# A two-layer decoder trunk: both mixings in finer steps and new orders, and the MLP up product with both parts of x side by side

## The chip, the core and the metric

The kernel runs on one core of one Trainium2 chip. Its time is the device time of one execution in microseconds; 694.61 is the median of three runs. One more execution was taken with the hardware profiler.

## What is computed

One sequence of 256 tokens, width 1024, in float32, goes through two layers and a final norm. Each layer is a mixing and an MLP, each added to x.

```python
for l in range(2):
    z = rms_norm(x, ln_mix[l]) @ w_in[l]
    u_self, q_mem = z[..., :768], z[..., 768:]
    if l == 0:
        self_out = s5_mixer(u_self, ...)      # 48 groups of 16 channels, 64 complex states, then a gated GELU
    else:
        k, v = rope(rms_norm(x, kv_norm) @ w_kv)   # 12 heads of 64
        self_out = causal attention of rope(u_self) over k, v
    mem_out = attention of q_mem (4 heads) over 256 memory tokens, their k, v = rms_norm(mem) @ w_mem_kv[l]
    x = x + concat(self_out, mem_out) @ w_out[l]
    up = causal depthwise conv, width 3, of (rms_norm(x) @ w_up[l])   # 2 x 2816 channels: g, v
    x = x + (silu(g) * v) @ w_down[l]
return rms_norm(x, final_norm)
```

## The kernel before

x is held on chip with its channels on the partitions (8 blocks of 128 by 256 tokens). The weights come by DMA in one fixed order through three raw buffers (class `Stream`). Most products keep float32 accuracy by splitting: ScalarE rounds a weight block to `whi` (line 115), VectorE makes the rest `wlo` (line 119, or 121 where a gain is multiplied in), the activations are split the same way, and `mm3` (lines 249 to 251) multiplies whi with hi, whi with lo and wlo with hi. Weights named in `NATIVE` are not split: they are multiplied as float32, for which the trace shows two instructions to a product. Five pairs of whi and wlo are held at a time.

The first mixing (`layer0`) has these steps, each a letter of the string `ORDER`: P the input product in float32 (line 869), E the powers of the poles, X the input operators (two halves, r and i, for three thirds b = 0, 1, 2 of the channels), T and t their transposes (line 771), V the output operators (array `Vd`), l a local operator that TensorE builds (lines 838 and 841) and L its placing by ScalarE into `Tm`, u and U the input moved to its place, S the states (products at lines 896 and 897, then rotation, scan and rotation back on VectorE, giving `Hs`), Y the outputs (lines 941 and 944, then transposes), G the GELU, K and K1 the memory's keys and values of layer 0 and layer 1 (lines 377 and 381), m the split of the memory for K1, A the four memory heads. Constants such as `E_POOL`, `X_POOL`, `H_DVE`, `U_ACT` say which engine does which piece. TensorE, VectorE and GpSimd issue the steps of `ORDER` exactly in that order. The gate product, the product with w_out and the additions to x follow, ordered by the framework's planner, which puts what is ready first by its place in the program.

`ffn` runs 22 passes: pass f makes two blocks of up channels in one PSUM bank `psU` (48 matmuls of 256 columns), `post` evacuates it, multiplying with the norm `rb` (line 521), convolves (526, 528), gates (532 to 534) and splits (541); from pass 5 on the down product of pass f - 5 follows (24 matmuls of 256 columns in layer 0, 12 of 512 columns at line 557 in layer 1). The banks alternate between two pairs, so four passes can be in flight. The norm enters only at line 521, so TensorE starts before it is known.

The second mixing (`layer1`) has its steps in `ORDER1`: I the input product, X the split for keys and values, K and v these, Q and R the rotary embeddings, h0 to h3 the memory heads, h4 to h15 the causal heads (scores, softmax, transposes at line 458, product with v at lines 470 and 471), O the output product, z the additions to x. Here the planner decides, and the string gives priorities. A head's product with v fills one half of the partitions of its pair's bank.

## Time and profile before

| | |
|---|---|
| median of 3 runs | 694.61 us (694.43 to 701.04) |
| profiled execution | 695.04 us, span 693.3 |
| TensorE matmul busy | 654.1 us, 94% of the span |
| VectorE busy | 565.4 us, 82% |
| ScalarE busy | 413.2 us, 60% |
| GpSimd busy | 132.9 us, 19% |
| mean granted TensorE clock | 0.957 |

PE is TensorE's matmuls, PEld its weight loads, DVE VectorE, ACT ScalarE, POOL GpSimd. Matmuls overlap each other, so how dense TensorE is shows in the distance between their starts, not in the busy time. The granted clock is a share of 2.4 GHz; 0.5 is 1.2 GHz.

### The profile page before, as it was taken

Reading aid. Unit: us, or ns where it says so; the run is one execution under the profiler, and the core shown is the slowest. Engines: PE = TensorE matmul, PEld = TensorE weight load, DVE = VectorE, ACT = ScalarE, POOL = GpSimd, SP = SyncE. Lnnn points to the kernel's source line nnn. Section 1 sums busy time; section 2 is a strip of 40 time slices with the busy share of each in tenths; the row PEclk is TensorE's granted clock in tenths of the full one; section 3 lists DMA queues with packets and bytes.
Section 4 is the critical chain, followed back from the end, with each engine's and each line's share of the span. In section 5 each row is a group of like instructions: output and inputs, shape, how many; then the busy total and the mean of one; then the engine's idle time right before and its main releaser. Section 6 shows DMA issues by size and latency. Waiting matters only on the chain.

```text
span 693.3 us, 12668 instructions
## 1 busy us (share of the span) xinstructions
PE 654.1 (94%) x4904; PEld 616.5 (89%) x4904; DVE 565.4 (82%) x1012; ACT 413.2 (60%) x747; POOL 132.9 (19%) x134
## 2 busy tenths in 40 slices
PE   6369899999999999999999998989999999999995
PEld 5358888998899999999999997868999999999984
DVE  7996999796879998888888798974749999888872
ACT  6368625576556665555557579864636666555631
POOL 5795623402300000000001255500300000000000
PEclk9775879999999999999999999899999999999998
DMA  8610133274455555555555544323625555565401
GB/s 315 245 62 1 61 99 99 93 217 148 152 181 184 183 183 181 186 185 182 182 186 156 168 128 140 107 89 122 213 92 182 181 186 183 183 188 187 172 1 61
DMA packets 43259, 105.13 MB, mean 152 GB/s; under 512 B 3776, under 2 KB 14144, under 8 KB 43200
## 3 DMA queue, kind: packets, MB, share of 16 engines
q1 hardware_dynamic: 42624, 103.74, 45.9%
q8 instruction: 38, 0.62, 0.4%
q10 hardware_dynamic: 576, 0.59, 0.2%
q14 instruction: 21, 0.17, 0.1%
HBM read 103.28 MB, written 1.05 MB: 150 GB/s over the span
## 4 chain that ended last, share of the span: by engine, by line
PE 82%; DVE 12%; DMA 2%; issue 2%; ACT 1%; POOL 0%; SPq 0%; DVEq 0%; ACTq 0%
PE psU L250 12%; PE psU L251 12%; PE psU L249 12%; PE acc L557 9%; PE acc L249 7%; PE acc L250 7%; PE acc L251 7%; PE ps L377 2%; DVE wlo L119 2%; PE ps L381 2%; PE ps L838 1%; DMA s5c<-s5b 1%; PE psO L470 1%; DVE X L638 1%; PE psT L458 1%
## 5 line engine op out<-in xcount | busy, mean ns | idle before, releaser
L115 ACT ACTIVATE whi<-wraw 128x1024 fp32r<-128x1024 f32 (+1 forms) x176 | 182.9, 1042 | 142.4 <-PE psU L250 84.9
L119 DVE TENSOR_TENSOR wlo<-wraw,whi 128x1024 fp32r<-128x1024 f32 (+1 forms) x176 | 217.9, 1240 | 26.7 <-PE acc L251 13.1
L250 PE MATMUL psU<-xlo,whi 128*128 128x256 f32 x704 | 198.6, 282 | 1.4 <-DVE xlo L331 1.4
L251 PE MATMUL psU<-xhi,wlo 128*128 128x256 f32 x704 | 197.8, 282 | 0.0
L249 PE MATMUL psU<-xhi,whi 128*128 128x256 f32 x704 | 197.6, 282 | 0.0
L250 PEld LDWEIGHTS psU<-xlo,whi 128*128 128x128 f32 x704 | 132.9, 189 | 2.5 <-DVE xlo L331 1.8
L249 PEld LDWEIGHTS psU<-xhi,whi 128*128 128x128 f32 x704 | 132.7, 189 | 0.7
L251 PEld LDWEIGHTS psU<-xhi,wlo 128*128 128x128 f32 x704 | 132.6, 189 | 0.0
L528 DVE SCALAR_TENSOR_TENSOR y<-u,held,y 128x254 f32<-128x254 f32 (+1 forms) x176 | 77.8, 477 | 1.5 <-ACT y L526 1.5
L521 DVE TENSOR_TENSOR u<-psU,rb 128x512 f32<-128x512 f32 x44 | 30.3, 688 | 32.4 <-PE psU L251 31.3
L526 ACT ACTIVATE y<-u,held 128x256 f32<-128x256 f32 x88 | 47.6, 589 | 13.0 <-DVE u L521 12.9
L269 POOL TENSOR_TENSOR sq<-sq 128x512 f32<-128x512 f32 x5 | 8.0, 1598 | 226.9 <-DVE held L364 179.1
L251 PE MATMUL acc<-ah,wlo 128*128 128x256 f32 x176 | 49.7, 283 | 0.0
L250 PE MATMUL acc<-al,whi 128*128 128x256 f32 x176 | 49.7, 283 | 0.0
L249 PE MATMUL acc<-ah,whi 128*128 128x256 f32 x176 | 49.6, 282 | 0.0
L869 PE MATMUL acc<-xg,wraw 128*128 128x256 f32 x128 | 34.1, 429 | 5.5 <-ACT xg L859 5.5
L869 PEld LDWEIGHTS acc<-xg,wraw 128*128 128x128 f32 x128 | 27.7, 221 | 10.0 <-ACT xg L859 5.5
L288 POOL TENSOR_TENSOR y<-mf,held 128x1 f32<-128x1 f32 x2 | 1.1, 550 | 180.5 <-DVE mf L1215 180.5
L249 PEld LDWEIGHTS acc<-ah,whi 128*128 128x128 f32 x176 | 33.6, 191 | 0.0
L251 PEld LDWEIGHTS acc<-ah,wlo 128*128 128x128 f32 x176 | 33.5, 191 | 0.0
L250 PEld LDWEIGHTS acc<-al,whi 128*128 128x128 f32 x176 | 33.5, 191 | 0.0
L250 PE MATMUL acc<-xlo,whi 128*128 128x256 f32 x112 | 31.7, 284 | 0.0
(271 smaller groups left out, 1475.1 us busy)
## 6 DMA issues: line engine op xcount, KB each, us to landing
wraw<-w_up SPq DMA_DIRECT2D x88, 512.0 KB, 3.4
wraw<-w_down SPq DMA_DIRECT2D x44, 512.0 KB, 3.4
wraw<-w_out SPq DMA_DIRECT2D x16, 512.0 KB, 3.6
wraw<-w_in SPq DMA_DIRECT2D x15, 512.0 KB, 3.5
wraw<-w_mem_kv SPq DMA_DIRECT2D x8, 512.0 KB, 4.2
wraw<-w_kv SPq DMA_DIRECT2D x6, 512.0 KB, 3.7
wraw<-w_kv SPq DMA_DIRECT2D x8, 384.0 KB, 3.4
wraw<-w_glu SPq DMA_DIRECT2D x6, 384.0 KB, 3.5
```

The lines of the kernel that those rows point to most:

```text
L115: self.nc.scalar.activation(hi[:, c], t[:, c], AF.Copy, scale=1.0 if g_ is None else g_)
L119: self.nc.vector.tensor_sub(lo[:, c], t[:, c], hi[:, c].bitcast(F32))
L249: PE.matmul(out, whi, ahi, start=first, stop=False, skip_group_check=True)
L250: PE.matmul(out, whi, alo, start=False, stop=False, skip_group_check=True)
L251: PE.matmul(out, wlo, ahi, start=False, stop=last, skip_group_check=True)
L377: PE.matmul(pk[:, 256 * m:256 * m + 256], w[i][:, o + 128 * m:o + 128 * m + 128], g[j], start=k + m + i + j == 0, stop=k == KT - 1, skip_g ...
L381: PE.matmul(pv[:, 256 * t:256 * t + 256], g[j][:, 128 * t:128 * t + 128], w[i][:, o + 256:o + 512], start=k + t + i + j == 0, stop=k == KT ...
L521: V.tensor_mul(u, v2(p), rb2(rb))
L526: S.activation(y[:, j], u[:, j], AF.Identity, bias=cp(3), scale=cp(2))
L528: V.scalar_tensor_tensor(y[:, j, d:], u[:, j, :T - d], cp(2 - d), y[:, j, d:], op0=ALU.mult, op1=ALU.add)
L557: PE.matmul(dacc[2 * t + h], a_, w_[:, 512 * i:512 * i + 512], start=False, stop=last and a_ is al, skip_group_check=True)
L869: PE.matmul(acc[2 * h + b][:, 256 * (m % 2):256 * (m % 2) + 256], w[:, 512 * i + 128 * m:512 * i + 128 * m + 128], xg[k // 2][:, k % 2], s ...
```

## The change

- First mixing: a new `ORDER`, with smaller steps (P in halves, l in quarters, each head in four steps with a separate step p for its pair's product with v, the gate product, the output product and the additions in the string too). Behind the bar in the string the planner decides. The weights are streamed in the order of the steps that use them.
- First mixing, engines: all but one of the V operations move from GpSimd to VectorE; three of the four rounds of E1 stay on GpSimd, the fourth goes to VectorE and the fourth round of E0 to GpSimd; one X half is on GpSimd as before, another one; eight of twelve placing copies of U on VectorE go to ScalarE; two evacuations of the transposes and three of Y come to VectorE; all H additions are on VectorE.
- K1 is multiplied in float32: its weights and the memory are no longer split.
- The narrow products of S, Y and l are reordered, so that neighbours go to different column groups of the array; S is cut into halves of 64 columns. The operand `dd` of l is prepared on the host.
- Attention: both heads of a pair are multiplied with v in one step, alternating.
- MLP: in passes 1 to 4 `normalise` makes two blocks each of x times gain times norm, split into hi and lo that lie side by side. From pass 5 on one matmul of 512 columns multiplies whi with both, and one of 256 wlo with hi. Each block of up channels then has a bank of its own, and ScalarE copies one half and VectorE adds the other (no multiplication with the norm).
- Second mixing: a new `ORDER1`, softmax in two steps, one rotary stack moved from GpSimd to VectorE.

```diff
@@ -29,11 +29,13 @@
-NATIVE = (("mkv", 0), ("win", 0))
+NATIVE = (("mkv", 0), ("mkv", 1), ("win", 0))
...
+
+NORMED = 5
...
-P rm0 E0 P rx1 E1 P rx2 E0 P rx3 Xi0 Xr0 E0 V1 u0 t0 V0 V0 Xi1 u1 P B0 T0 D0 V0 Xr1 V1 U1 U0 P U0 l0 U0 T1 E1 U0 E1
-E1 Xi2 Xr2 E0 U1 S0 V1 P t2 S0 T2 S0 L0 U1 L0 P B1 L0 V2 t1 S0 D1 u2 U1 V2 U2 U2 U2 m S1 U2 S2 K S1 K K D2 K rm1 V2
-S1 B2 q l1 S1 L1 L1 rm2 L0 S2 Y0 S2 m S2 K K K K rm3 Y0 K L1 L1 G0 m K1 Y1 G0 Y2 Y1 K1 K1 m Y2 K1 G1 G2 K1 K1 G1 K1
-A G2 A A A A K1 A K1 A
+P E0 P P E1 P P P rm0 E0 Xr0 rx1 P P P rx2 E0 rx3 E0 E1 P Xi0 u0 D0 P U0 T0 U0 P U0 t0 P E1 D2 Xr1 P U0 V0 B0 Xi1 S0
+u1 V0 V0 l0 T1 Xi2 U1 S0 P U1 S0 l0 V2 V1 P V1 L0 V2 t1 K Xr2 B1 S0 L0 T2 U1 K u2 V1 rm1 U2 K U2 U1 L0 L0 Y0 B2 K U2
+t2 U2 E1 S1 V2 l1 D1 l1 l1 l1 L1 rm2 L1 S1 rm3 S2 Y0 S1 S1 K L1 K S2 K S2 Y0 L1 S2 K K1 Y1 K G0 G0 | q Y2 Y2 h1 Y1 h2
+Y1 h1 h3 h3 K1 K1 h0 Y2 h2 G1 h1 G2 h0 K1 K1 h0 K1 G1 h2 G2 h3 h1 h2 h0 K1 h3 K1 g g g g g p1 g0 g0 g g1 p0 g1 p1 K1
+g2 p0 o o o o g2 o o o o z3 z2 z1 z0
 """
-X_POOL = ((0, 1),)
-E_POOL = (1,)
-M_POOL = (1, 2, 3)
-H_DVE = (1,)
-V_DVE = ()
-Y_ACT = (0, 1, 2)
-EVAC_ACT = (0, 1, 2)
-T_ACT = ((0, 0), (0, 1), (1, 0), (1, 1), (2, 0), (2, 1))
-U_ACT = ((1, 1, 1, 0), (0, 1, 1, 1), (1, 0, 1, 1))
+V_POOL = ((2, 2),)
+X_POOL = ((2, 0),)
+E_POOL = ((0, 3), (1, 0), (1, 1), (1, 2))
+H_DVE = (0, 1, 2)
+Y_ACT = (1,)
+EVAC_ACT = (0, 2)
+T_ACT = ((0, 0), (0, 1), (1, 1), (2, 0), (2, 1))
+U_ACT = ((1, 1, 1, 0), (1, 1, 1, 1), (1, 1, 1, 1))
...
+x x x x I I I X r1 r2 I I I I r3 I X Q0 qm Q1 K K Q1 h0 K X h3 X h2 Q2 K h1 h0 K h2 h2 R0 h1 h2 v Q0 R1 v R0 h3 R1 v
+h0 h3 h1 K Q2 h10 h7 h0 h1 h5 v R2 h4 h3 h5 h4 h4 h7 v v h8 h5 h4 h11 h6 h10 h9 v v p0 h6 e0 h9 h10 h6 R2 h13 h5 p1 h7
+h8 h14 h8 h7 h8 h12 h6 p1 p0 e1 h10 h9 h12 O h11 p3 h13 h12 h12 h9 h15 h11 p3 h13 h14 h11 h15 h14 p4 p5 h13 h15 p2 p2
+p5 p4 p6 O h14 O h15 p7 p6 p7 O z0 O O O O z3 z2 z1
...
+    def mem_kv(l, bk, mem, ks, new, vm):
...
+                PE.matmul(pk[:, 256 * m:256 * m + 256], w[:, o + 128 * m:o + 128 * m + 128], mk, start=k + m == 0,
+                          stop=k == KT - 1, skip_group_check=True)
             for t in range(2):
-                for i, j in pairs:
-                    PE.matmul(pv[:, 256 * t:256 * t + 256], g[j][:, 128 * t:128 * t + 128],
-                              w[i][:, o + 256:o + 512], start=k + t + i + j == 0, stop=k == KT - 1,
-                              skip_group_check=True)
...
+    def pv(out, pair, causal):
+
+        for t in range(2):
+            c = 128 if t and causal else 0
+            for h in range(2):
+                v, PT = pair[h]
+                PE.matmul(out[64 * h:64 * h + 64, c:256], v[t], PT[:, t, c:], start=t == 0, stop=t == 1,
+                          skip_group_check=True)
...
+    def head_pair(i, bo, causal, outp, hi, lo):
+
+        po = bo("psO")
+        pv(po, [outp.pop(2 * i + h) for h in range(2)], causal)
+        yield
+        o = po[:, :256]
+        S.activation(hi[i], o, AF.Copy)
+        V.tensor_sub(lo[i], o, hi[i].bitcast(F32))
+        yield
...
+            def normalise(b):
+
+                t = sg([128, 2, T], name="xn")
+                for i in range(2):
+                    k = 2 * b + i
+                    V.scalar_tensor_tensor(t[:, i], x[:, k], gains[:, gi, k:k + 1], rb, op0=ALU.mult, op1=ALU.mult)
+                for i in range(2):
+                    n = sn([128, 2, T], F32R, "xhl")
+                    S.activation(n[:, 0], t[:, i], AF.Copy)
+                    V.tensor_sub(n[:, 1], t[:, i], n[:, 0].bitcast(F32))
+                    hl.append(n)
+
             def post(f, p):
                 u = sl([128, 2, T], name="u")
-                V.tensor_mul(u, v2(p), rb2(rb))
+                if f < NORMED:
+                    V.tensor_mul(u, v2(p), rb2(rb))
+                else:
+                    for j in range(2):
+                        S.activation(u[:, j], p[j][:, T:], AF.Copy)
+                        V.tensor_add(u[:, j], p[j][:, :T], u[:, j])
                 y = sl([128, 2, T], name="y")
                 for j in range(2):
                     c = j * FT + f
@@ -558,15 +583,20 @@
                                   stop=last and a_ is al, skip_group_check=True)
             for f in range(FT):
-                p = (br if f % 2 else bw)("psU")
-                w = [None, None]
-                todo = [(j, k) for j in range(2) for k in range(KT)]
-                for j, k in todo:
-                    if w[j] is None:
-                        w[j] = W.get(("up", l, j * FT + f))
-                    c = slice(128 * k, 128 * k + 128)
-                    mm3(p[:, 256 * j:256 * j + 256], w[j][0][:, c], w[j][1][:, c], *act(k),
-                        k == 0 and j == 0, k == KT - 1)
+                p = (br if f % 2 else bw)("psU") if f < NORMED else [b_("psU") for b_ in (br, bw)]
+                for j in range(2):
+                    whi, wlo = W.get(("up", l, j * FT + f))
+                    for k in range(KT):
+                        c = slice(128 * k, 128 * k + 128)
+                        if f < NORMED:
+                            mm3(p[:, 256 * j:256 * j + 256], whi[:, c], wlo[:, c], *act(k), k == 0 and j == 0, k == KT - 1)
+                        else:
+                            PE.matmul(p[j], whi[:, c], hl[k].rearrange("p a t -> p (a t)"), start=k == 0, stop=False,
+                                      skip_group_check=True)
+                            PE.matmul(p[j][:, :T], wlo[:, c], hl[k][:, 0], start=False, stop=k == KT - 1,
+                                      skip_group_check=True)
+                if 0 < f <= 4:
+                    normalise(f - 1)
                 post(f, p)
                 if LAG <= f < FT - 4 + LAG:
                     dacc = dacc or [ba("acc") for _ in range(4)]
...
         def local_operator(i):
             n, nf = LEN[i], LEN[i] // 4
             Tm[i] = s5.tile([128, n, 4, 32], F32, name=f"Tm{i}")
             G.memset(Tm[i], 0.0)
-            dds = []
-            for q in range(n // 8):
-                d = sv([128, 8, 32], name="dd")[:32]
-                V.tensor_mul(d, ident[:32, None, :32].to_broadcast([32, 8, 32]),
-                             dsk[:, PC[i][0] + 8 * q:PC[i][0] + 8 * q + 8, None].to_broadcast([32, 8, 32]))
-                dds.append(d)
-            p = ba()
+            p = pl[i] = ba()
             for f in range(nf):
+                o = [p[32 * s:32 * s + 32, 128 * f:128 * f + 128] for s in range(4)]
+                for g in range(2):
+                    for s in range(4):
+                        PE.matmul(o[s].rearrange("p (i c) -> p i c", c=32)[:, :, 16 * g:16 * g + 16],
+                                  Bz[i][:, 4 * f + s, g], Vd[i][:, 4 * f + s, g, 0:4], start=g == 0, stop=False,
+                                  tile_position=(0, 32 * s), skip_group_check=True)
                 for s in range(4):
-                    pr = 4 * f + s
-                    o = p[32 * s:32 * s + 32, 128 * f:128 * f + 128]
-                    for g in range(2):
-                        PE.matmul(o.rearrange("p (i c) -> p i c", c=32)[:, :, 16 * g:16 * g + 16],
-                                  Bz[i][:, pr, g], Vd[i][:, pr, g, 0:4], start=g == 0, stop=False,
-                                  tile_position=(0, 32 * s), skip_group_check=True)
-                    PE.matmul(o[:, :32], ident[:32, :32], dds[pr // 8][:, pr % 8], start=False, stop=True,
-                              tile_position=(0, 32 * s), skip_group_check=True)
-            pl[i] = p
+                    PE.matmul(o[s][:, :32], ident[:, 32 * s:32 * s + 32], dsk[:, PC[i][0] // 4 + f], start=False,
+                              stop=True, tile_position=(0, 32 * s), skip_group_check=True)
+                yield
...
@@ -893,8 +915,10 @@
             i, o = piece(b)
             pr, pi = br(), br()
             for j in range(8):
-                PE.matmul(pr[:, 64 * j:64 * j + 64], RT[b][0][:, j], U[b][:, j], start=True, stop=True)
-                PE.matmul(pi[:, 64 * j:64 * j + 64], RT[b][1][:, j], U[b][:, j], start=True, stop=True)
+                for ri, p in enumerate((pr, pi)):
+                    for c in HALF:
+                        PE.matmul(p[c, 64 * j:64 * j + 64], RT[b][ri][:, j, c], U[b][:, j], start=True, stop=True,
+                                  tile_position=(0, c.start), skip_group_check=True)
             yield
             ec, es = E[i][:, 0, o:o + 8], E[i][:, 1, o:o + 8]
             rt = lambda: sr([128, 8, 64], name="rot")
...
@@ -934,21 +958,23 @@
         def outputs(b):
             pc, off = piece(b)
             py = ba("psY")
-            for f in range(2):
-                for s in range(4):
-                    j = 4 * f + s
-                    o = py[64 * f:64 * f + 64].rearrange("p (i s c) -> p s i c", s=4, c=32)[:, s]
-                    PE.matmul(o, U[b][:, j], Tm[pc][:, off + j], start=s == 0, stop=False, tile_position=(0, 64 * f),
-                              skip_group_check=True)
-                    for g in range(2):
-                        PE.matmul(o[:, :, 16 * g:16 * g + 16], Hs[b][:, j, g], Vd[pc][:, off + j, g, 1:5],
-                                  start=False, stop=True, tile_position=(0, 64 * f), skip_group_check=True)
+            for s in range(4):
+                o = [py[64 * f:64 * f + 64].rearrange("p (i s c) -> p s i c", s=4, c=32)[:, s] for f in range(2)]
+                for f in range(2):
+                    PE.matmul(o[f], U[b][:, 4 * f + s], Tm[pc][:, off + 4 * f + s], start=s == 0, stop=False,
+                              tile_position=(0, 64 * f), skip_group_check=True)
+                for g in range(2):
+                    for f in range(2):
+                        PE.matmul(o[f][:, :, 16 * g:16 * g + 16], Hs[b][:, 4 * f + s, g],
+                                  Vd[pc][:, off + 4 * f + s, g, 1:5], start=False, stop=True,
+                                  tile_position=(0, 64 * f), skip_group_check=True)
             yield
             yc = sx([128, 4, 128], name="yc")
...
```

## Rows read from the trace of the kernel before

**Rows 1.** TensorE by time, first mixing: start us, us, line, operation, out<-in, [idle before <-releaser].

```profile
15.97 7.15 PE L869 MATMUL acc<-xg,wraw 128*128 128x256 f32 x32
...
36.69 1.97 PE L771 MATMUL ps<-held,X 128*128 128x128 f32 x8 [11.75 <-DVE X L638]
...
51.65 0.31 PE L841 MATMUL ps<-dd,held 32*32 32x32 f32 x2 [4.07 <-DVE dd L829]
...
183.07 0.28 PE L249 MATMUL psU<-xhi,whi 128*128 128x256 f32 x1
```

**Rows 2.** Stretches: us, then PE, PEld, DVE, ACT, POOL busy (count), clock, DMA, GB/s.

```profile
40.00:60.00 20.00, 15.94 (x97) 12.93 (x97) 19.20 (x42) 16.73 (x45) 12.24 (x26) 0.76 0.17 53
...
300.00:340.00 40.00, 40.00 (x338) 40.00 (x337) 32.70 (x53) 21.85 (x32) 0.00 (x0) 1.00 0.57 185
...
420.00:440.00 20.00, 16.82 (x89) 15.24 (x89) 18.54 (x26) 19.07 (x38) 12.69 (x12) 0.83 0.41 132
```

**Rows 3.** VectorE and GpSimd in order of time, first mixing.

```profile
29.10 4.66 POOL L635 TENSOR_TENSOR Vd<-s5c 128x1024 f32<-128x1024 f32 x2
...
32.01 4.62 DVE L638 TENSOR_TENSOR X<-xt 64x512 f32<-64x512 f32 x2
...
54.14 1.41 DVE L638 TENSOR_TENSOR X<-xt 64x512 f32<-64x512 f32 x2
```

**Rows 4.** VectorE's groups by shape, first MLP: count | busy us, mean ns | idle before.

```profile
L119 DVE TENSOR_TENSOR wlo<-wraw,whi 128x1024 fp32r<-128x1024 f32 x66 | 80.5, 1220 | 10.6 <-PE psU L251 5.5 <-PE acc L251 4.2 <-issue 0.6
...
L521 DVE TENSOR_TENSOR u<-psU,rb 128x512 f32<-128x512 f32 x22 | 15.1, 688 | 14.3 <-PE psU L251 13.3 <-ACT rb L308 1.0
```

**Rows 5.** VectorE's groups by shape, first mixing.

```profile
L121 DVE SCALAR_TENSOR_TENSOR wlo<-wraw,held,whi 128x512 fp32r<-128x512 f32 x8 | 9.6, 1246 | 0.0
```

**Rows 6.** TensorE in order of time, the S5 layer's narrow products.

```profile
78.01 0.33 PE L896 MATMUL ps<-U,RT 128*128 128x64 f32 x2
...
81.75 0.39 PE L897 MATMUL ps<-U,RT 128*128 128x64 f32 x2
...
99.97 0.41 PE L838 MATMUL ps<-Vd,Bz 128*32 128x64 f32 x4
...
108.29 0.43 PE L941 MATMUL psY<-Tm,U 128*64 128x128 f32 x2
...
109.92 0.22 PE L944 MATMUL psY<-Vd,H 128*64 128x64 f32 x1
109.92 0.32 PE L941 MATMUL psY<-Tm,U 128*64 128x128 f32 x1
...
111.87 1.13 PE L377 MATMUL ps<-memT,wraw 128*128 128x256 f32 x4
```

**Rows 7.** TensorE in order of time, one pass of the second MLP.

```profile
567.42 0.62 PE L557 MATMUL acc<-whi,ah 128*128 128x512 f32 x2
...
570.20 0.28 PE L249 MATMUL psU<-xhi,whi 128*128 128x256 f32 x1
...
575.90 0.62 PE L557 MATMUL acc<-whi,ah 128*128 128x512 f32 x2
```

**Rows 8.** The page's DMA issues: count, KB each, us to landing.

```profile
wraw<-w_mem_kv SPq DMA_DIRECT2D x8, 512.0 KB, 4.2
```

**Rows 9.** TensorE in order of time, attention, second mixing.

```profile
461.31 0.65 PE L470 MATMUL psO<-PT,vv 128*64 128x256 f32 x2
...
462.10 0.55 PE L458 MATMUL psT<-held,P 128*128 128x128 f32 x3
...
473.75 0.66 PE L470 MATMUL psO<-PT,vv 128*64 128x256 f32 x4
...
474.56 0.55 PE L458 MATMUL psT<-held,P 128*128 128x128 f32 x3
```

**Rows 10.** VectorE in order of time, the start of either MLP.

```profile
213.60 1.37 DVE L528 SCALAR_TENSOR_TENSOR y<-u,held,y 128x255 f32<-128x255 f32 x3 [0.69 <-ACT y L526]
...
515.56 0.69 DVE L521 TENSOR_TENSOR u<-psU,rb 128x512 f32<-128x512 f32 x1 [5.51 <-PE psU L251]
```

More of the change, by code (lines that the diff above doesn't have):

```diff
@@ L198, in _body, with by_steps @@
     W0 = [((0,), 0), ((1,), 0)] + [(ks, h) for h in range(2) for ks in PAIRS][1:]
[L199 to L205 removed]
+    def by_steps(steps, **lists):
+        its = {n: iter(l) for n, l in lists.items()}
+        return [w for s_ in steps.split() if s_ in its for w in next(its[s_], ())]
+    one = lambda l: [[w] for w in l]
+    w0 = [(("win", 0, ks, h), blocks(a["w_in"][0], ks, 512 * h, 512), (len(ks), 512)) for ks, h in W0]
+    mkv = lambda l: [[(("mkv", l, k // 2), mkv_ap(l, k // 2), (2, 512))] if k % 2 == 0 else [] for k in range(KT)]
+    glu = [(("glu", ks, b), blocks(a["w_glu"], ks, 256 * b, 256), (3, 256)) for ks, b in GLU]
+    order = by_steps(ORDER, P=[w0[:2], []] + [p for w in w0[2:] for p in ([w], [])], K=mkv(0), K1=mkv(1), g=one(glu),
+                     o=one(wout(0)))
+    order += ffn_order(0)
+    order += by_steps(
+        ORDER1, I=one(win(1)),
+        K=one([(("wk", ks, b), blocks(a["w_kv"], ks, 256 * b, 256), (4, 256)) for ks, b in WK]),
+        v=one([(("wv", ks, c), blocks(a["w_kv"], ks, SELF + 384 * c, 384), (2, 384)) for c in range(2) for ks in PAIRS]),
+        O=one(wout(1)))
+    order += ffn_order(1)
     W = Stream(nc, order, rawp, hlp, lambda key: [gains[:, 2 + key[1], 2 * key[2] + i:2 * key[2] + i + 1]
@@ L1050, in layer0, with steps @@
                 calls[f"{n}{b}"] = lambda f=f, b=b: f(b)
+        gens["g"], gens["o"] = gate(), output0()
+        for b in range(3):
+            gens[f"g{b}"] = gated(b)
+        for b in range(4):
+            calls[f"z{b}"] = lambda b=b: residual0(b)
         for i in range(2):
-            calls[f"l{i}"] = lambda i=i: local_operator(i)
+            gens[f"l{i}"] = local_operator(i)
             gens[f"L{i}"] = put_local_operator(i)
-        with tc.manual_schedule(engines=MANUAL):
-            for s in ORDER.split():
+        def steps(text):
+            for s in text.split():
                 if s in gens:
@@ L1091, in layer1 @@
         causal_ops.extend([identb, maskb])
-        act, d = split_x(1), {}
+        sq_, d = [], {}
+        act = split_x(1, steps=sq_)
         rb = pool.tile([128, T], F32, name="rbq")
```

176 lines of the change are left out of this document (73 added, 103 removed).

## Prediction

> **What bounds the kernel now.** I read the stretches of the span first, then each engine in order of time within a stage, then the groups by shape. The reader is to see four stages with different limits. The first mixing lasts until the first `psU` matmul at 183.1 us [rows 1]. TensorE stands still 11.75 us before its first transpose at 36.7 and 4.07 us before line 841 at 51.65 [rows 1]; from there to 183.1 its matmuls follow each other almost without a gap, but dear ones: the granted clock averages 0.76 of full speed between 40 and 60 us [rows 2]. VectorE is busy 19.2 of 20 us there, so both engines are near their limit. The MLPs are TensorE's alone: 40.0 of 40 us at full clock, VectorE at 32.7, ScalarE at 21.9 [rows 2]. In the second mixing TensorE is at 16.8 of 20 us in the worst stretch and VectorE and ScalarE at 18.5 and 19.1 [rows 2]: there they set the pace. So a gain must come from less TensorE time in the first mixing and the MLPs, and from an earlier start.
>
> **First mixing, the start.** TensorE's first transposes wait for X. The pair of X writes at 32.0 takes 4.62 us beside GpSimd's V products; the same pair at 54.1, with GpSimd idle, 1.41 [rows 3]. V (2.33 us each on GpSimd [rows 3]) leaves GpSimd, which removes most of that neighbour, while both halves of the first X now stand on VectorE. I take the difference of this pair, 3.2 us, as the earlier start. Bounds: 0, if the extra half and the rounds of E left on GpSimd eat it; 6, if the other operations of that stretch shrink too.
>
> What VectorE gains and loses: eight V operations of 1024 elements a partition at 1.22 (line 119 has that size [rows 4]) are 9.8 us more; the eight splits of K1's weights are 9.6 us less [rows 5]. The smaller moves (a round of E, H, five evacuations in; copies of U, the split of the memory, `dd` out) are shorter operations on both sides, and I count them even. VectorE therefore stays at its present sum, less what GpSimd's presence cost it, in a stage that gets shorter.
>
> **First mixing, TensorE's narrow products.** S: 30 instructions from 78.01 to 81.75 are 0.125 us each, so 32 take 4.0. Y: 48 instructions from 108.29 to 111.87 take 3.58. l: 96 instructions from 99.97 to 108.29 take 8.3, and the first, half as long, 4.2 at the same clock [rows 6]. In all of them neighbours now lie on the same columns of the array. The one place in Y where the column half changes shows two matmuls with one start, 109.92 [rows 6]: different column groups run side by side. With neighbours alternating, Y's halves overlap throughout: 1.8 instead of 3.6, three times, saves 5.4. S becomes 64 half-wide instructions; at Y's mean of 3.58 / 48 = 0.075 each they would cost 4.8, overlapped 2.4 or less; I take 2.0, three times, saving 6.0 (bounds: 2.4 lost to 6.0 saved). l has four column groups: 12.5 us falls to 3.1 if all four overlap, to 6.2 if two do; I take 4.5, saving 8.0 (bounds 0 to 9.4). `dd` and TensorE's wait for it go; the next late thing there is V on VectorE, so I credit nothing.
>
> K1 in float32 has 32 products of two instructions each at 7.15 / 32 = 0.223 [rows 1]: 14.3 us, against 96 split ones at 5.70 / 48 = 0.119 [rows 7]: 11.4. That costs 2.9. Its weights now stay in the three raw buffers until they are multiplied, and what is loaded behind them waits for that; a block lands in 4.2 us [rows 8] and its share of the 14.3 is 3.6, so with two blocks ahead the loads keep up: 0. The memory heads: one head's product with v takes 0.79 us (461.31 to 462.10), both of a pair side by side 0.81 (473.75 to 474.56) [rows 9]. Two pairs save 1.6. Sum: 5.4 + 6.0 + 8.0 + 1.6 - 2.9 = 18.1 us of TensorE time.
>
> What TensorE saves counts only if it doesn't wait instead. Y0 now stands ahead of the last two thirds of l, S1 and S2 in TensorE's fixed order; it waits for Hs[0], which VectorE makes after V0, four more V operations, Xr1, Xi1 and Xi2, and K, t2, S1, l1 and S2 wait behind Y0. I keep the sum of waits and slow stretches as it is. Bounds: at 0.76 about half of 40 to 60 us, 9.6 us, ran at 1.2 GHz, which cost 4.8, and the wait before line 841 cost 4.07 [rows 1, 2]; as much again, or none of it, is 9 us either way. First mixing: 3.2 + 18.1 = 21.3 us less, so its end comes near 162.
>
> **Second mixing.** Eight pairs are multiplied with v together where three are now (473.75 is the first of these), so five pairs save 0.8 each; two of the five are memory heads in the stretch where VectorE and ScalarE set the pace [rows 2], where it hides. Three count: 2.4. The rotary stack on VectorE adds to the engine that is late there, the finer softmax steps only change priorities. Bounds: 9 us gained, if the new order fills the holes, 5 lost.
>
> **MLP.** A pass has 48 matmuls of 256 columns in 570.20 to 575.90: 0.1188 each; 512 columns take (570.20 - 567.42) / 12 = 0.232 [rows 7]. The new pass has 16 of each: 16 x (0.232 + 0.1188) = 5.61 against 5.70. That is 0.09 us a pass, 3.2 over 2 x 17 passes: two halves side by side are almost as long as two matmuls. Bounds 0 to 6.
>
> Here the Trainium skill would give another number: its page "TensorE: Matmul & The Clock Gate", section "Back-to-back issue gap", has 512 columns at about 131 ns in a sustained stream with weight loads. By that a pass would take 16 x (131 + 119) = 4.0 us, 58 us less over the 34 passes; no run here shows it, and the row has 232.
>
> `post` now has two VectorE additions of 256 elements out of PSUM in place of one of 512 (0.688 [rows 4]): between 0.69 and 1.38 together. A pass of 8.5 us has 32.7 / 40 x 8.5 = 7.0 us of VectorE work [rows 2], so even the upper end fits: 0. ScalarE has 40 - 21.9 of 40 us free [rows 2], 3.9 a pass, for two copies of 256 elements: 0 too.
>
> `normalise` adds four VectorE operations of 256 elements in each of passes 1 to 4: from half of 0.688 each [rows 4], 5.5 us, to 11 at its full price. Pass 5 on TensorE needs them all. In the first MLP VectorE has no free time for them: from the norm at 199 to the end of pass 4 near 215 it idles once, 0.69 us at 213.60 [rows 10]; behind it are the splits of the next weights and the evacuations. TensorE can go on with the down product meanwhile, so I charge 3 us (0 to 7). In the second MLP VectorE stands idle 5.51 us before its first evacuation at 515.56 [rows 10], which takes the 5.5: 0 (0 to 6).
>
> **Sum.** -21.3 - 2.4 - 3.2 + 3.0 = -23.9 us. The profiled execution took 695.0 us (693.3 of span, 1.7 around it), 0.4 over the median; 694.6 - 23.9 = 671.
>
> **Rivals.** (1) Freed time turns into waiting: TensorE comes to Y0 and to the gate product sooner than VectorE, and idles at the lower clock. For it: VectorE's 19.2 of 20 us, and the clock of 0.76 [rows 2] around the 4.07 us wait [rows 1]. Of the 18.1 some 12 are lost: 683. (2) The waits go too, as the order is finer and GpSimd no longer slows VectorE: the 9 us above and as much again of the 11.75 us [rows 1], some 16 in all: 655. (3) The column groups don't overlap beyond what the trace shows once: S 2.4 dearer, Y and l unchanged, that is 21.8 us off the gain: 693, no change. Against it: the equal starts [rows 6] and pairs of heads [rows 9]. (4) Slower: from pass 5 on a pass holds two banks, so two passes are in flight in place of four, and the copy, the addition and the splits must keep time. Once a pass takes over 8.49 + 23.9 / 34 = 9.2 us instead of TensorE's 8.49, the whole gain is gone; at 9.6 it is 34 x 1.1 = 37.7 us, 709. Against it: 1.5 us of VectorE's time is free in every pass [rows 2]. (5) The wide matmuls overlap each other, so that the up product shrinks until VectorE's 7.0 us a pass bound it: 34 x 1.5 = 51 us, 620. Against it: twelve such matmuls at 0.232 in the pass [rows 7]. The skill's rule above is what would bring it about.
>
> **How the numbers follow.** Forecast 0.56, (1) 0.18, (2) 0.13, (3) 0.06, (4) 0.06, (5) 0.01. A measurement of this kernel can tell about 1%, 7 us, from no change. Faster by more than that (below 687.7): the forecast, (1), (2) and (5), 0.88. Within: (3), 0.06. Slower: (4), 0.06. The range takes in the forecast with its bounds, most of (2) and (1): 650 to 688. The likeliest case and its neighbours have one sign.
>
> **What the new profile would show.** Right: the first `psU` matmul near 162; S at about 2 us, Y at 1.8 and l's two at 4.5 together, with equal starts on different columns; X unslowed at 1.4; up passes of 5.6 us; the first transpose near 33. Wrong: a gap ahead of Y0 of over 10 us with 1.2 GHz behind it; a stall at pass 5 of either MLP; more us than now from the first `psU` matmul of one MLP to that of the other. The prediction fails most easily on the waits of the first mixing, which I have carried over unchanged.

## The result and the profile after

The changed kernel takes 670.26 us (median of four runs, 669.94 to 671.23), the kernel before 694.83 (694.43 to 701.04): a ratio of 0.963, with a 95% interval of 0.957 to 0.968. 671 was predicted. Runs of the kernel before fall into two groups, near 695 and near 700 us, so a ratio moves by some tenths of a per cent with how many of each it was taken against. The profiled execution took 670.0 us, 668.3 of it span, and the clock granted over the whole span rose from 0.957 to 0.98.

Stage by stage I read the first `psU` matmul of either MLP and the last matmul of the first one's down product, TensorE in order of time (us; "first mixing" ends where the first `psU` matmul starts):

| kernel | first mixing | first MLP | second mixing | second MLP |
|---|---|---|---|---|
| before | 183.1 | 191.9 | 121.8 | 196.5 |
| changed | 163.3 | 190.8 | 118.4 | 195.8 |
| forecast of the difference | -21.3 | +1.4 | -2.4 | -1.6 |
| difference | -19.8 | -1.1 | -3.4 | -0.7 |

TensorE by time in the changed kernel (start, us, line, out<-in, count, idle before), the rows that answer to [rows 1, 6, 7]:

```profile
34.16 1.04 PE L800 MATMUL ps<-held,X 128*128 128x128 f32 x8
...
73.76 0.48 PE L968 MATMUL psY<-Vd,H 128*64 128x64 f32 x4 [8.42 <-DVE H L950]
...
81.06 2.40 PE L920 MATMUL ps<-U,RT 128*64 128x64 f32 x64
83.39 0.43 PE L859 MATMUL ps<-Vd,Bz 128*32 128x64 f32 x16
83.64 0.24 PE L863 MATMUL ps<-dsk,held 128*32 128x32 f32 x8
83.70 0.41 PE L859 MATMUL ps<-Vd,Bz 128*32 128x64 f32 x16
...
163.28 0.28 PE L262 MATMUL psU<-xhi,whi 128*128 128x256 f32 x1
...
306.03 0.39 PE L594 MATMUL psU<-xhl,whi 128*128 128x512 f32 x1
306.26 0.28 PE L596 MATMUL psU<-xhl,wlo 128*128 128x256 f32 x1
306.37 0.39 PE L594 MATMUL psU<-xhl,whi 128*128 128x512 f32 x1
```

The first transposes start 2.5 us earlier in this profile (in the ten builds with this start they begin at 34.2 to 35.9 us, on average 1.5 us earlier). S takes 2.3 us (81.06 to 83.39) where it took 4.0. A quarter of the local operator, 24 instructions, takes 0.31 us (83.39 to 83.70), so all six quarters take about 2 us where 12.5 went. The wide MLP matmul has its neighbour 0.23 us behind it, the narrow one 0.11. And TensorE stands still 8.42 us in front of Y0, at the place that the prediction named.

The stretches of both kernels from 60 to 120 us, before first (us, then busy time and count of PE, PEld, DVE, ACT, POOL, the granted clock, DMA, GB/s):

```profile
60.00:120.00 60.00, 58.13 (x376) 51.67 (x376) 53.12 (x68) 30.71 (x69) 30.00 (x26) 0.82 0.23 70
```

```profile
60.00:120.00 60.00, 42.70 (x520) 37.31 (x520) 57.56 (x83) 29.16 (x62) 12.97 (x13) 0.91 0.24 73
```

TensorE had no time left there and now idles 17.3 of 60 us; VectorE has become the full engine. The chain of waits says the same. From 20 to 125 us its pieces add up to 55.1 us of TensorE and 42.4 of VectorE in the kernel before, 10.7 and 78.4 in the changed one, where 9.2 more are ScalarE's, most of them its copies of U from 75.86 to 81.0. A stretch of it (start, us, what):

```profile
65.36 2.27 DVE vt L667 x2
...
68.23 2.37 DVE rot L941
...
75.14 0.70 DVE uT L899
75.86 0.31 ACT U L908
...
81.49 1.88 PE ps L920 x56
83.39 0.69 DVE rot L927
```

So two theories stand against each other. **The prediction's**: the first mixing got shorter by the TensorE time that was taken out of it, less its waits. **The rival**: VectorE carries the changed kernel from some 20 to 118 us; TensorE's time counted only until VectorE was full, and what VectorE itself was rid of counts too.

### The profile page after: what moved, and what is told of

Same layout as the page of the kernel before. It is cut to its first block, busy times and chain, and to the rows that moved or that the text cites. A ratio compares the mean times of both kernels' runs of the same rounds, so it can differ in the third digit from the quotient of the medians.

```text
span 668.3 us, 11710 instructions
## 1 busy us (share of the span) xinstructions
PE 620.8 (93%) x4424; PEld 562.6 (84%) x4424; DVE 564.4 (84%) x1077; ACT 433.5 (65%) x830; POOL 105.7 (16%) x117
## 4 chain that ended last, share of the span: by engine, by line
PE 74%; DVE 19%; ACT 3%; issue 2%; DMA 0%; POOL 0%; DVEq 0%; ACTq 0%; POOLq 0%
PE psU L594 19%; PE psU L596 10%; PE acc L582 9%; PE acc L263 7%; PE acc L264 7%; PE acc L262 7%; PE psU L264 3%; PE psU L262 3%; PE psU L263 3%; DVE wlo L121 3%; DVE X L667 1%; DVE xt L667 1%; PE psO L483 1%; DVE cf L674 1%; PE psT L467 1%
## 5 line engine op out<-in xcount | busy, mean ns | idle before, releaser
L121 DVE TENSOR_TENSOR wlo<-wraw,whi 128x1024 fp32r<-128x1024 f32 (+1 forms) x176 | 213.6, 1217 | 26.6 <-PE psU L596 9.2
L594 PE MATMUL psU<-xhl,whi 128*128 128x512 f32 x544 | 192.1, 395 | 0.0
L596 PE MATMUL psU<-xhl,wlo 128*128 128x256 f32 x544 | 152.5, 280 | 0.0
L594 PEld LDWEIGHTS psU<-xhl,whi 128*128 128x128 f32 x544 | 102.1, 188 | 22.7
L596 PEld LDWEIGHTS psU<-xhl,wlo 128*128 128x128 f32 x544 | 102.9, 189 | 0.7
L264 PE MATMUL psU<-xhi,wlo 128*128 128x256 f32 x160 | 45.1, 283 | 0.4 <-DVE wlo L121 0.4
L262 PE MATMUL psU<-xhi,whi 128*128 128x256 f32 x160 | 44.9, 284 | 0.0
L263 PE MATMUL psU<-xlo,whi 128*128 128x256 f32 x160 | 44.6, 282 | 0.0
L545 ACT ACTIVATE u<-psU 128x256 f32<-128x256 f32 x68 | 24.4, 373 | 18.9 <-PE psU L596 18.9
L546 DVE TENSOR_TENSOR u<-psU,u 128x256 f32<-128x256 f32 x68 | 27.7, 418 | 9.8 <-ACT u L545 9.8
```

The lines of the kernel that those rows point to most:

```text
L121: self.nc.vector.tensor_sub(lo[:, c], t[:, c], hi[:, c].bitcast(F32))
L262: PE.matmul(out, whi, ahi, start=first, stop=False, skip_group_check=True)
L263: PE.matmul(out, whi, alo, start=False, stop=False, skip_group_check=True)
L264: PE.matmul(out, wlo, ahi, start=False, stop=last, skip_group_check=True)
L546: V.tensor_add(u[:, j], p[j][:, :T], u[:, j])
L594: PE.matmul(p[j], whi[:, c], hl[k].rearrange("p a t -> p (a t)"), start=k == 0, stop=False, skip_group_check=True)
```

## The experiments

Comparisons between variants go by their own medians (the changed kernel: 670.3), the ratios by the runs of the kernel before on the same chip. Behind the part that is ordered by hand a planner orders the rest, so a stage that an edit doesn't touch can move between the profiles: the first mixing, untouched in the third and fourth experiment, took 163.0 and 165.7 us, and 167.6 in the tenth. A difference of under 3 us between two variants is therefore read here together with rows of the operations that the edit changed, not from the total alone.

**1. The narrow products in their old order.**

```diff
-                for ri, p in enumerate((pr, pi)):
-                    for c in HALF:
-                        PE.matmul(p[c, 64 * j:64 * j + 64], RT[b][ri][:, j, c], U[b][:, j], start=True, stop=True,
-                                  tile_position=(0, c.start), skip_group_check=True)
+                PE.matmul(pr[:, 64 * j:64 * j + 64], RT[b][0][:, j], U[b][:, j], start=True, stop=True)
+                PE.matmul(pi[:, 64 * j:64 * j + 64], RT[b][1][:, j], U[b][:, j], start=True, stop=True)
...
-                for g in range(2):
-                    for s in range(4):
+                for s in range(4):
+                    for g in range(2):
...
-            for s in range(4):
-                for f in range(2):
+            for f in range(2):
+                for s in range(4):
```

> The changed kernel with its state products (S), output products (Y) and local operators (l) put back into the order and shape of the kernel before; all else stays changed. TensorE gets back about 2.0 us for each of three S, 1.8 for each of three Y and 10 for the local operators, some 21 us. Theory: in the changed kernel VectorE and not TensorE carries the chain from 25 to 118 us, so only a part of the 21 comes back at the end: the start of S1 moves by some 3 to 5 us, the local operator of the second piece (7 us) and S2 stand behind it, and VectorE has about 11 us of its own work to cover them: about 10 us, 680 us (677 to 684). First rival: TensorE's time is the stage's time, and all of it comes back: 689 to 692 us. Second rival: the interleaving is worth nothing and the new order alone made the gain: 670 us, within 1.5.

Measured: 673.31 us (0.965, 0.961 to 0.970), first mixing 166.5. Only 3 us come back, less than any bound of mine for this theory; the first rival (689) is out, and the second (670 within 1.5) is missed by 1.8 us. The rows show why it is so little. S and Y are dear again, but the local operator is not (TensorE by time; a pair of its tiles repeats every 0.14 us):

```profile
86.60 0.30 PE L859 MATMUL ps<-Vd,Bz 128*32 128x64 f32 x4
86.71 0.22 PE L862 MATMUL ps<-dsk,held 128*32 128x32 f32 x2
86.74 0.30 PE L859 MATMUL ps<-Vd,Bz 128*32 128x64 f32 x4
```

That is 23 ns an instruction; the kernel before had 87 in the same order [rows 6]. The order by itself, with 128 rows throughout, does not make it slow.

**2. The interleaved products in the kernel before.** The edit of 1 the other way round, in the kernel before, with its own diagonal product of 32 rows.

> The kernel before with only the interleaved S, Y and local operators of the changed one; order, engines and MLP stay as before. Theory (VectorE becomes the bound as soon as TensorE's time is freed): VectorE is idle for 6.9 us of the stretch from 60 to 120 us in which these products lie, so about 7 to 10 us are gained: 686 us (684 to 689). First rival, TensorE's time is the stage's time: 19 to 21 us gained, 675 us. Second rival, interleaving gives nothing: 695 us within 1.5.

Measured: 689.58 us (0.989, 0.984 to 0.993), 5 us faster, half a microsecond beyond the theory's range and far from the 675 of TensorE's bookkeeping. From 60 to 120 us:

```profile
60.00:120.00 60.00, 43.86 (x479) 38.27 (x479) 58.09 (x67) 32.55 (x73) 34.77 (x32) 0.80 0.23 73
```

Against the same stretch of the kernel before, TensorE is rid of 14.3 us, VectorE rises from 53.1 to 58.1 of 60, and the stage gains 2.9 (the rest of the total lies in the first MLP, which the edit doesn't touch: 189.1 us for 191.9). The freed time became waiting, as rival (1) of the prediction has it.

**3. The old MLP.**

```diff
-NORMED = 5
+NORMED = 22
...
-                if 0 < f <= 4:
-                    normalise(f - 1)
```

> The changed kernel with the MLP up product of the kernel before in all passes: three products of 256 columns, no wide one, no normalised x. Theory from the stage lengths of the two traces (first MLP 1.07 us shorter, second 0.74): 672 us, 1.8 above the changed kernel. The sum of the prediction (wide products 3.2 us gained, normalising 3 us lost in the first MLP) gives 670.5. Rival: the MLP's change costs time and is hidden in the total: below 669.

**4. The old MLP, and x normalised for nothing.** `NORMED = 22` alone: `normalise` runs in passes 1 to 4 and no product reads its result.

> The changed kernel with the MLP up product of the kernel before in all passes, but x is still normalised and split in the first passes of both MLPs (16 us of VectorE and ScalarE work whose result no product reads). Against the same kernel without normalising this is the price of normalising alone. Theory (the prediction's term): 3 us, all of it in the first MLP, so 675 us if the other is at 672. Rival: it hides under TensorE's passes: equal to the other within 0.5 us.

Measured: 669.99 us (0.961, 0.958 to 0.965) and 670.65 (0.961, 0.957 to 0.966). The MLP's change is worth nothing that can be measured: the prediction's sum (670.5) held and the 1.8 us read from two traces did not. Normalising by itself costs 0.7 us in the total and 0.9 in the first MLP (190.3 us against 189.4), not 3: the theory is out. The stages show a cancellation. Over all kernels measured here the first MLP takes 190.4 to 192.6 us with wide passes (eight of them, mean 191.6) and 189.1 to 190.2 without wide passes and normalising (four, mean 189.5; the kernel before, whose MLP starts with a wait, 191.9). The second takes 195.2 to 196.1 wide (nine, mean 195.6, and one of 197.3) and 196.2 to 197.8 narrow (four, mean 196.8). So it loses 2 us in the first and gains about 1 in the second. Where the 2 us go, stretches of 25 us from about 40 us into the first MLP, the changed kernel and then the one of experiment 3:

```profile
203.30:228.30 25.00, 22.88 (x150) 20.62 (x149) 24.53 (x49) 17.60 (x34) 0.00 (x0) 1.00 0.46 157
```

```profile
203.00:228.00 25.00, 25.00 (x212) 25.00 (x212) 23.11 (x42) 14.45 (x23) 0.00 (x0) 1.00 0.54 192
```

VectorE is full in the first, and TensorE idles 2.1 us of the 25; in the second it never does. Normalising alone (experiment 4) left TensorE at 25.0 too. So the idle time appears where passes that normalise are followed by wide passes that ask for their result at once; wide passes without normalising were not run.

**5. Old order, and the diagonal product with 32 rows.** As 1, with the shape of the kernel before at the one product that it had otherwise:

```diff
+            for s in range(4):
+                S.activation(dd[:, s], dsk[32 * s:32 * s + 32], AF.Copy)
...
-                    PE.matmul(o[s][:, :32], ident[:, 32 * s:32 * s + 32], dsk[:, PC[i][0] // 4 + f], start=False,
+                    PE.matmul(o[s][:, :32], ident[:32, :32], dd[:, s, PC[i][0] // 4 + f], start=False,
```

> The changed kernel with S, Y and local operators in the order of the kernel before, as in the first experiment, and also with the diagonal product of the local operator in the shape of the kernel before (32 rows of weights where the changed kernel contracts over 128; the diagonal tiles are copied to rows 0 to 31 by ScalarE, early). In the kernel before a product of the local operator took 87 ns at full clock (96 in 8.33 us), with 128 rows in the same order it took 26 (96 in 2.53 us). If the change of row count between products is what cost that time, the 96 take 8 us again, S2 stands 5.5 us later, and VectorE, which in the first experiment had 4.4 us of cover there, is late by 1 to 3 us: 676 us (674 to 679). Rival, the slow local operator of before came from elsewhere: 96 products in 2.5 us, 673 us. Second rival, TensorE's time is the stage's time: 691 us.

Measured: 679.01 us (0.971, 0.968 to 0.975), first mixing 172.0: the theory, at the slow edge of its range. TensorE by time, and below it VectorE where it waits:

```profile
87.39 0.41 PE L862 MATMUL ps<-Vd,Bz 128*32 128x64 f32 x4
87.74 0.24 PE L865 MATMUL ps<-dd,held 32*32 32x32 f32 x2
87.91 0.41 PE L862 MATMUL ps<-Vd,Bz 128*32 128x64 f32 x4
```

```profile
87.28 0.69 DVE L927 TENSOR_TENSOR rot<-ps,E 128x512 f32<-128x512 f32 x1 [4.00 <-PE ps L920]
99.67 0.69 DVE L927 TENSOR_TENSOR rot<-ps,E 128x512 f32<-128x512 f32 x1 [1.33 <-PE ps L920]
```

A pair of tiles repeats every 0.52 us again, against 0.14 with 128 rows: going from 128 rows to 32 and back costs 0.38 us a time in this order. The changed kernel changes the row count nowhere in it, and that takes away the price. But the price is not a fixed one. In experiment 2 the product keeps its 32 rows; there the four column groups alternate and the eight small instructions of a quarter stand together, so that the row count changes and comes back once in a quarter and not four times:

```profile
50.64 0.43 PE L837 MATMUL ps<-Vd,Bz 128*32 128x64 f32 x16
51.01 0.26 PE L842 MATMUL ps<-dd,held 32*32 32x32 f32 x8
```

With the next transposes starting at 51.20, this quarter takes 0.55 us at full clock; the same quarter of the changed kernel takes 0.42 (47.11 to 47.53), and one in the old order 2.06 (four pairs of 0.52). One change and back costs 0.13 us here, a third of the price above. Either edit alone, 128 rows (0.57 to 0.83 a quarter in experiment 1) or the interleaved order, takes away most of what the old local operator cost. The Trainium skill has the rule, on its page "TensorEngine Tiling (Array Packing)", section "Key Properties": changing the tiling mode, as opposed to the tile, drains the array. The rows agree that the change has a price; that the array drains, and what sets the amount, they do not show. All narrow products together are worth 8.7 us at the end (679.0 against 670.3).

**6. H0 earlier, and 7. Y0 later.** Both go at TensorE's wait of 8.42 us, one from VectorE's side and one from TensorE's:

```diff
-... U1 S0 P U1 S0 l0 V2 V1 P V1 L0 V2 t1 K Xr2 B1 S0 L0 T2 ...
+... U1 S0 P U1 S0 l0 S0 V2 V1 P V1 L0 V2 t1 K Xr2 B1 L0 T2 ...
```

> The changed kernel with the last step of S0 (the states H0, 7 us on VectorE) moved ahead of the output operators V2, V1 in VectorE's order. H0 then comes 4.4 us earlier or more, and TensorE's wait of 8.4 us at Y0 shrinks by as much. Theory (VectorE carries the chain from 25 to 118 us, and the order of its own work changes nothing): 670 us, within 1 of the changed kernel. Rival (TensorE's wait at Y0 is what the stage loses): 666 us.

```diff
-... L0 L0 Y0 B2 K U2
-t2 U2 E1 S1 V2 l1 D1 ...
+... L0 L0 B2 K U2
+t2 U2 E1 S1 Y0 V2 l1 D1 ...
```

> The changed kernel with the output product Y0 moved behind the state product S1 in TensorE's order. The wait for H0 is then passed by S1, and S1's states come when U1 and the transposed operator are there. Theory (VectorE is the bound): VectorE waited only 1.0 us for S1 (at 83.39 us) and 0.8 for a root before it, so 1 us is gained: 669 us (668.5 to 670.5). Rival (TensorE's wait is the loss): 4 to 8 us gained, 662 to 666.

Measured: 670.33 (0.959, 0.955 to 0.962) and 669.63 (0.957, 0.954 to 0.961). With H0 early no wait is left at Y0, and TensorE waits for VectorE elsewhere instead (the next places by time):

```profile
76.11 0.43 PE L859 MATMUL ps<-Vd,Bz 128*32 128x64 f32 x16 [0.98 <-DVE Vd L667]
81.54 1.22 PE L314 MATMUL ps<-held,y 128*128 128x128 f32 x4 [4.07 <-DVE y L307]
```

With Y0 late the waits at Y0 are 3.23 and 1.07 us in place of 8.42 and 0.92. The longest wait of the stage cost nothing that can be measured. TensorE's bookkeeping (666, 662 to 666) is out for this stretch.

**8. The memory's sum of squares on TensorE.**

```diff
-            d["pm"] = sums(d["sm"], ba)
+            p = d["pm"] = ba()
+            for t in range(2):
+                for k, s_ in enumerate(d["sm"]):
+                    for h in range(2):
+                        PE.matmul(p[:, t:t + 1], s_[:, 256 * h + 128 * t:256 * h + 128 * t + 128], ones,
+                                  start=k + h == 0, stop=k == 3 and h == 1)
```

> The changed kernel with the sums of squares of the memory (three additions of 128 x 512 on GpSimd, 57 to 62 us) done by TensorE: 32 products of one column instead of 8, in its wait ahead of Y0. Theory (VectorE is the bound there, and it is slowed beside GpSimd: an addition of states takes 1.75 us beside these sums and 0.68 elsewhere, the two scans 2.29 and 2.22 against 1.22 and 1.20): VectorE gets back 3.2 us, 667 us (666 to 668.5). First rival: the scans are slow for another reason, or TensorE's wait is the bound: 670 us. Second rival: the 24 added products at 130 ns each, at half clock, delay the products behind them by 3 us: 671 to 673.

Measured: 667.06 us (0.954, 0.951 to 0.957), the theory's number. VectorE in the changed kernel, then here:

```profile
55.35 1.73 DVE L931 TENSOR_TENSOR rot<-rot 128x512 f32<-128x512 f32 x1
57.00 1.75 DVE L932 TENSOR_TENSOR rot<-rot 128x512 f32<-128x512 f32 x1
58.68 2.29 DVE L935 TENSOR_TENSOR_SCAN rot<-dec,rot 128x512 f32<-128x512 f32 x1
60.89 2.22 DVE L936 TENSOR_TENSOR_SCAN rot<-dec,rot 128x512 f32<-128x512 f32 x1
```

```profile
54.77 1.71 DVE L931 TENSOR_TENSOR rot<-rot 128x512 f32<-128x512 f32 x1
56.41 0.68 DVE L932 TENSOR_TENSOR rot<-rot 128x512 f32<-128x512 f32 x1
57.01 1.21 DVE L935 TENSOR_TENSOR_SCAN rot<-dec,rot 128x512 f32<-128x512 f32 x1
58.14 1.19 DVE L936 TENSOR_TENSOR_SCAN rot<-dec,rot 128x512 f32<-128x512 f32 x1
```

Three operations, beside which GpSimd made its additions from 56.79 to 62.02 us, get 3.2 us back when it falls silent, and the end moves by 3.2. TensorE's 24 added products went into its wait.

**9. V on GpSimd again.** `V_POOL` holds all nine steps.

> The changed kernel with all nine steps of the output operators on GpSimd, as in the kernel before (the changed one has eight of them on VectorE). VectorE is rid of 9.5 us of work of its own (three steps of V0 3.7 us, three of V1 3.5, two of V2 2.3). Theory (VectorE carries the first mixing, and an operation of VectorE of 128 x 512 with two tensors read from the on-chip buffer waits while GpSimd runs: beside the one step of 2.35 us that GpSimd has now, VectorE's product took 2.45 us against 0.68, that is 1.8 us lost to 2.35): eight steps of 2.35 us more cost VectorE 14 us, so 5 us net, and the local operators start later: 676 us (673 to 682). Rival (no contention, VectorE simply rid of work): 9.5 us gained, 661. Second rival (VectorE is not the bound): 670.

Measured: 674.36 us (0.966, 0.961 to 0.971), first mixing 168.3: in the theory's range, and the 661 of a VectorE that is simply rid of work is out. It is not contention alone. VectorE and GpSimd by time:

```profile
54.35 0.69 DVE L805 COPY RT<-ps 128x512 f32<-128x512 f32 x1 [11.47 <-PE ps L800]
54.96 3.07 DVE L667 TENSOR_TENSOR xt<-s5c 128x512 f32<-128x512 f32 x2
58.06 4.63 DVE L667 TENSOR_TENSOR X<-xt 64x512 f32<-64x512 f32 x2
```

```profile
50.01 2.37 POOL L664 TENSOR_TENSOR Vd<-Vd,vt 128x1024 f32<-128x1024 f32 x1
```

The local operator waits for V0, which GpSimd finishes at 52.4, the next transposes stand behind it on TensorE, and VectorE behind these for 11.5 us; after that the X pair takes 4.63 us beside V, where it took 1.41 alone [rows 3]. VectorE's busy time in the stage falls from 142.7 to 137.9 us, 4.8, though the steps that left it add up to 9.5 in the expectation: by that difference the contention took about as much again.

**10. Wide passes in the second MLP alone.** `NORMED = (22, 5)`, by layer.

> The changed kernel with the wide up product and the normalised x in the second MLP alone; the first has the passes of the kernel before. Stage lengths so far: the first MLP takes 190.8 us wide and 189.4 narrow, the second 195.8 wide and 197.8 narrow. Theory of the prediction (wide products gain 1.6 us in each MLP, normalising costs the first MLP 3 us of waits and the second nothing): 668.7 us. Rival: the two stage lengths are scatter and the MLP's change moves nothing in either: 670.3 us within 1.

Measured: 675.41 us (0.967, 0.962 to 0.972), slower than either theory. The MLPs aren't the place: the first mixing, whose order wasn't edited, took 167.6 us. ScalarE and VectorE by time:

```profile
36.57 0.39 ACT L1040 ACTIVATE rb<-ps 128x256 f32<-128x256 f32 x1 [2.43 <-POOL E L664]
```

```profile
36.99 0.69 DVE L899 TENSOR_TENSOR uT<-acc,rb 128x512 f32<-128x512 f32 x1 [3.19 <-ACT rb L1040]
```

In this build the copy of `rb` waits for TensorE and for GpSimd, in the changed kernel for TensorE alone; VectorE waited 0.78 us there. That accounts for 2.4 of the 4.3 us that this first mixing is longer. The rest, and why the build set the wait (that a buffer fell on another place is my guess), stays open. As a test of the MLP the run says little.

**11. Both sums on TensorE.** As 8, with the sum of x too.

> The changed kernel with both sums of squares of the first mixing on TensorE instead of GpSimd: that of the memory, as in the earlier run at 667.1 us, and that of x (18.4 to 22.3 us on GpSimd, beside which VectorE's small products took 1.24 and 0.68 us each where one of that shape elsewhere takes 0.2 to 0.3). Theory (VectorE carries the stage from 18 us on and is held up beside GpSimd): another 2.5 us are gained, 664.5 us (664 to 666). Rival: VectorE's early work has slack, since the first transposes wait for other things: 667 us, as with the memory's sum alone.

Measured: 664.94 us (0.953, 0.949 to 0.957), 2.1 more. VectorE in the changed kernel, beside GpSimd's sum, then here:

```profile
18.52 1.24 DVE L771 TENSOR_TENSOR s5c<-cf 128x24 f32<-128x24 f32 x1
19.79 2.73 DVE L756 TENSOR_TENSOR ct<-s5c 128x48 f32<-128x48 f32 x4
```

```profile
18.90 0.18 DVE L771 TENSOR_TENSOR s5c<-cf 128x24 f32<-128x24 f32 x1
19.10 0.56 DVE L756 TENSOR_TENSOR ct<-s5c 128x48 f32<-128x48 f32 x4
```

**12. The edits together.** 11, with Y0 late as in 7, `V_POOL = ()`, and the MLPs of 10.

> The kernel with both sums on TensorE (664.9 us) with three more edits: Y0 behind S1 in TensorE's order, the last step of V2 on VectorE instead of GpSimd, and the wide up product in the second MLP alone. Theory, VectorE carries the first mixing: its wait of 1.6 us for S1 (which stands behind Y0) goes, and V2's step costs 1.2 us there but gives back the 1.8 us that a product of the rotation loses beside it, 0.6 net: the first mixing ends 2.2 us earlier. The first MLP has the narrow passes, 1.5 us shorter by the stage lengths (189 to 190 against 190 to 192). In all 661.2 us (660 to 663). Rival: the waits for S1 and beside GpSimd only change places, and the MLP's stages scatter: 665 us.

Measured: 661.25 us (0.947, 0.943 to 0.950), faster than both kernels. The total is the one expected, its parts are not quite: against 11 the first mixing is 1.1 us shorter (2.2 expected), the first MLP 1.1 (1.5 expected), and the second mixing and MLP, which the edits don't touch, 2.0. The product of the rotation that took 2.45 us beside V2's step takes 0.68 (61.87):

```profile
61.87 0.68 DVE L941 TENSOR_TENSOR rot<-rot,E 128x512 f32<-128x512 f32 x1
```

## Why the prediction was right, and where its reasons were not

**The first mixing, -21.3, measured -19.8.** The number held; the bookkeeping behind it held in part, and partly by luck. *Narrow products, -19.4*: TensorE's sizes were near (S 2.3 us for the 2.0 taken; the local operator 2 for 4.5, so 10 saved instead of 8; Y 1.9 where nothing waits, 102.84 to 104.70, for 1.8). The local operator's saving, though, was argued from the four column groups alone; the change of row count, which the prediction doesn't mention, was part of its old price (experiment 5).

"I keep the sum of waits and slow stretches as it is" came out as a sum, not as a reason. TensorE idles 24.7 us of the stage before (183.1 less 158.4 busy) and 31.3 now (163.3 less 132.0). At 1.2 GHz it is busy 33 us before and 10.5 now; the granted clock is 0.50 from 26.5 to 40.2, 50.4 to 70.9 and 84.5 to 94.8 us before, and from 23.8 to 27.2, 47.7 to 51.1 and 68.2 to 78.4 in the changed kernel. I estimate that half of that busy time is lost, since four of Y's products take 0.43 us there (75.43 to 75.86) and 0.22 at full clock (103.34 to 103.56). Waits and lost clock together are then 41 us before and 36.5 now, 5 less, where the forecast had 3.2 less for the start. That is a balance of two larger changes. In experiment 5, with the narrow products old and the rest new, the same sum is 27 (20.2 idle, and half of 14 busy at 1.2 GHz): the rest of the change took 14 us of it away, and the narrow products, 18 us of TensorE work, put 9 back as waiting, so that only 8.7 us of them reach the end. The prediction carried the sum over and sized neither.

*VectorE "stays at its present sum, less what GpSimd's presence cost it"* was right in kind, and I gave it no size: it is busy 142.7 us in the stage instead of 155.0, and what GpSimd cost it is a gain of its own. Putting V back costs 5.0 us of this stage, much of it by the wait for V0 (experiment 9). If the two reversals add, which no run shows, they are 13.7 of the 19.8; the other 6, the order, K1 and the smaller moves, I didn't take apart.

**The start, -3.2**: the first transposes came 2.5 us earlier in this profile, 1.5 on average over the ten builds with this start, and the X pair of 4.62 us [rows 3] now takes 1.41 at 26.03.

**K1, +2.9**: a row of the chain has 14 of its instructions in 3.02 us (119.24), 0.216 each for the 0.223 taken.

**Y0's wait** came as named, 8.4 us with the clock at 0.74 from 60 to 80. The prediction called that the place where it fails most easily. It cost nothing that can be measured (experiments 6 and 7): VectorE was the later engine.

**Second mixing, -2.4, measured -3.4**: 116.3 to 118.7 us in the twelve builds that have the new order and the paired heads (mean 117.8), 121.8 and 123.1 in the two that don't. The gain is real, 4 us, and larger than the term; which of its parts gave it was not tried.

**MLP.** A pass is 5.60 us (306.03 to 311.63) for the 5.61 taken. The change was forecast to lose 1.4 us in the first MLP (3 for normalising, 1.6 gained by the wide products) and to gain 1.6 in the second, and that holds in sign and nearly in size; the two terms in the first were not seen apart, and normalising without wide passes costs 0.9 there (experiment 4), not 3. The first MLP loses 2.1 with the change by the means above (the table's -1.1 comes from the kernel before, whose first MLP starts with TensorE busy 13.62 of 15 us), the second gains 1.2. That the two nearly cancel (-0.2 forecast) is why the change to the MLP neither helps nor harms.

**The rivals.** (1) happened by its mechanism: of 18 us of TensorE work in the narrow products 9 turned into waiting, and in experiment 2 11 of 14, but the rest of the change filled the place. (2) came in part: waits and lost clock fell by 5 us together where it had 16. (3), (4) and (5) didn't happen: groups overlap, passes keep time, and two wide matmuls stand 0.34 us apart with one narrow between them, so that the 131 ns of the Trainium skill's page "TensorE: Matmul & The Clock Gate", section "Back-to-back issue gap", aren't seen here.

## What to carry to other kernels

An engine that is busy 97% of a stretch is its bound only until the next one is full: read the idle time of the second engine there (6.9 us of VectorE's in 60) as the ceiling on what the first can give, before adding up its savings. A long wait of an engine that isn't on the chain can be worth nothing, as TensorE's 8.42 us here, and an edit that removes it can only move it elsewhere; taking 3 us off the engine that carries the chain gave 3 us. Where VectorE carries a stage, look for what GpSimd does beside it, and give that to an engine that waits.

## What the hardware showed that I had not expected

**GpSimd holds up VectorE for whole operations, and only some of them.** VectorE and GpSimd in the changed kernel:

```profile
67.55 0.68 DVE L805 COPY RT<-ps 128x512 f32<-128x512 f32 x1
68.15 2.45 DVE L941 TENSOR_TENSOR rot<-rot,E 128x512 f32<-128x512 f32 x1
70.53 0.68 DVE L942 TENSOR_TENSOR rot<-rot,E 128x512 f32<-128x512 f32 x1
71.13 0.68 DVE L943 TENSOR_TENSOR rot<-rot,E 128x512 f32<-128x512 f32 x1
```

```profile
67.71 2.35 POOL L664 TENSOR_TENSOR Vd<-Vd,vt 128x1024 f32<-128x1024 f32 x1 [5.68 <-DVE vt L667]
69.99 1.80 POOL L853 MEMSET Tm<- 128x2048 f32 x1
```

The product at 68.15 ends 0.5 us after GpSimd's operation does (70.06), as if it had begun only then. The copy out of PSUM beside the same operation, and the products beside GpSimd's memset, keep their 0.68. The Trainium skill states this on its page "SBUF — State Buffer", section "Who interferes with whom": a VectorE instruction with two inputs in SBUF contends with a GpSimd instruction that reads SBUF, not with one that only writes it; by the same section the contention is an exclusive lock on a shared pair of ports. The trace agrees in all three cases.

**Four column groups start almost together**: 96 instructions of the local operator take 1.28 us (83.39 to 84.67), 13 ns each, against 23 with neighbours in one group (experiment 1) and 87 with neighbours in one group and the row count changing between them.
